# Attention's first head: the last projection of the first stage in the other pair of PSUM banks, and the head's finishing work in another order

## The chip, the cores and the metric

The kernel runs on one core of a Trainium2 chip. The core has five engines that work from their own queues, each in order: TensorE (PE, matrix products), VectorE (DVE), ScalarE (ACT), GpSimd (POOL) and SyncE (SP); the last two here mostly issue transfers (DMAs). Matrix products are accumulated in PSUM, which has eight banks of 512 float32 columns on 128 partitions. What is measured is the time of one execution in microseconds; lower is better.

## The reference

The program is one layer of a decoder for 512 tokens of width 2048: an RMS norm, attention with 16 heads of 128 in four groups, a residual add, a second norm, a SwiGLU feed-forward, and a last norm. The attention has three branches, compressed, selected and windowed, which are merged with gates:

```python
proj = h @ w_in
q, kc, vc, ks, vs, kw, vw, gl = jnp.split(proj, bounds, axis=-1)
...
s_c = jnp.einsum('btghd,bcgd->bghtc', q, kcc) + bias_c
p_c = masked_softmax(s_c, mask_c)
...
o = gates[0] * o_c + gates[1] * o_s + gates[2] * o_w
return o.reshape(Bsz, S, N_HEADS * DH) @ w_out
```

With 512 tokens the eight selection blocks are all chosen and the window spans the sequence, so that the selected and the windowed branch are two causal attentions over all tokens, each with its own keys and values, and the compressed branch has 31 keys.

## The kernel before

Every product is made of three (`three`): both factors are split in a high and a low part, ACT making the high part by a copy and DVE the low part by a subtraction. A weight granule, 512 KB, is loaded, split (`Weights.split`: ACT writes `whi`, DVE then `wlo`) and taken (`Weights.take`). A take keeps the splits three granules ahead and the loads three more; so each take issues one split and then one load, at that place of the program.

The first stage (pool `ps1`, with `psx` beside it that lives on) makes the compressed keys and values, the keys and values of group 0 and the queries of heads 0 and 1. Its projections take two PSUM tiles at a time, `proj_tiles`, from `psx` and `ps1` in turn. The last of them is that of the first queries: `q_out` scales each half on DVE (`yt`, L319), has ACT write the high part (`qh`, L292) and DVE the low part (`ql`, L293). After it `ps1` is closed, and `ps2` opens over the same banks with the score tile `s` (three banks), two tiles for projections and one for the output `o`.

The second stage (`st2`) goes head by head. For each head h there are four token tiles t, longest first:

- `scores(h, t)`: PE multiplies queries and keys into `s` (L267 to L269). DVE adds the bias and takes the maxima (L800, `mx`), ACT makes the exponentials (L802).
- `finish(h, t)`: DVE scales by the sums and gates (L807 to L814) and transposes in 32 x 32 blocks (L815); SP writes the tile to DRAM in four transfers (`d_p`).
- `fetch(t)`: reads it back into `ptr`, turned. For head 0 this is issued from POOL, from head 1 on from SP.
- `turn(h, b, kt)`: ACT (L838, `pth`) and DVE (L842, `ptl`) split one key tile of one branch.
- `values(h, b, kt)`: PE multiplies it with the values into `o`.

Beside this runs a stream of independent projections, `dense()`: the next queries, keys and values, in steps of three 512-column products, each counted as 650 ns. `pump(h, step)` issues steps until their sum reaches a goal that grows by 20800 ns a head, 12 pump steps to a head, with a lead of four of these. Eight steps use up one granule of the queries in each fourth: steps 1, 9, 17 and 25 take one, and step 28 and step 32 end the two halves of a pair of queries (`q_out`). The first pair of the stream lies in `psx`. Its weights are loaded from POOL's queue, that of the fetches of head 0.

Ahead of the loop over heads, head 0 is started by hand: four passes, each of a `scores`, a `fetch`, a `finish` and a `pump`. In the loop, steps 0 to 8 each `turn` one tile, steps 2 to 11 multiply what was turned two steps before, and `scores` and `finish` of the next head stand at every third step. The program's order is the order in each engine's queue.

Of the kernel before, what the change touches and what calls it, by code (L numbers as in the profile page):

```python
# [10 lines left out]
F32 = mybir.dt.float32  # L11
# [162 lines left out]
def nsa_block(ctx: ExitStack, tc: tile.TileContext, x, rel_bias, mix_g, ffn_g, fin_g, w_in, w_out,  # L174
              pos_k, w1k, w2k, pos_v, w1v, w2v, f_in, f_out, onehot, out):
    nc = tc.nc
    mm, act, dve, pool = nc.tensor.matmul, nc.scalar.activation, nc.vector, nc.gpsimd
# [9 lines left out]
    psx = early.enter_context(tc.tile_pool(name="psx", bufs=2, space=PSUM))  # L187
# [17 lines left out]
    def tok(t):  # L205
        return slice(128 * t, 128 * (t + 1))
# [59 lines left out]
    def three(o, ah, al, bh, bl, start, stop):  # L266
        mm(o, ah, bh, start=start, stop=False, skip_group_check=True)  # L267
        mm(o, ah, bl, start=False, stop=False, skip_group_check=True)  # L268
        mm(o, al, bh, start=False, stop=stop, skip_group_check=True)  # L269
# [80 lines left out]
    with ExitStack() as st1:  # L350
        ps1 = st1.enter_context(tc.tile_pool(name="ps1", bufs=2, space=PSUM))

        turns = iter(range(1000))

        def proj_tiles(n=2):
            return [(ps1 if next(turns) % 4 > 1 else psx).tile([128, 512], F32, name="proj") for _ in range(n)]

        c0p = st1.enter_context(tc.tile_pool(name="c0p", bufs=1))
        posT = c0p.tile([128, 2, 32], F32, name="posT")
# [2 lines left out]
        with ExitStack() as st0:  # L362
# [90 lines left out]
            for k in range(4):  # L453
                scaled_in(k, ps[k])
            ps = proj_tiles()
            for q in range(4):
                it = ws(ps, q, W.take(0))
# [92 lines left out]
        for u in range(2):  # L550
            kv_out(ps_kc0, 0)(u)
        ps = proj_tiles()
        for i in range(4):
            run(ws(ps, i, W.take(), end=kv_out(ps, 2)))
            next(spread)
        ps = proj_tiles()
        for i in range(4):
            run(ws(ps, i, W.take()))
# [71 lines left out]
    with ExitStack() as st2:  # L630
# [112 lines left out]
        STEPS = 12  # L743

        def pump(h, step):
            at = h + (step + 4) / STEPS
            goal = 20800 * min(at, 13) + 22500 * max(at - 13, 0)
            while done["ns"] < goal:
                c = next(stream, "end")
                if c == "end":  # L750
                    return
                done["ns"] += c or 0
# [15 lines left out]
        def load_bias(h):  # L768
            if h < H:
                TB[h] = ap_.tile([128, S], F32, name="tb")  # L770
                (nc.sync if h else pool).dma_start(TB[h], bass.AP(tensor=d_u.tensor, offset=d_u.offset + h * UL + 127,
                                                 ap=[[H * UL - 1, 128], [1, S]]))

        def branch(t, b):

            return P[t][:, :, 32 * (t + 1) * b:32 * (t + 1) * (b + 1)]

        def scores(h, t):
            g, n = h // HPG, 128 * (t + 1)
            (qh, ql), (kh, kl) = Q[h], KK[g % 2]  # L780
            if t == NT - 1:
                HS[h] = dict(
                    mx=ap_.tile([128, NT, 3], F32, name="mx"), sm=ap_.tile([128, NT, 3], F32, name="sm"))
            s = HS[h]
            at = 224 + (512 if t == 1 else 0)
            cuts = [0, 288] + [c for c in (800, 1056) if c <= 32 + 2 * n]
            if cuts[-1] < 32 + 2 * n:
                cuts.append(32 + 2 * n)
            for c0, c1 in zip(cuts, cuts[1:]):
                three(sc[:, at + c0:at + c1], qh[:, tok(t)], ql[:, tok(t)], kh[:, c0:c1], kl[:, c0:c1], True, True)  # L790
            c = CX[t][:, :NCMP]
            regions = [(c, c, c, sc[:, at:at + NCMP], biasc[:, h, 24 - 8 * t:24 - 8 * t + NCMP])]
            bt = TB[h][:, S - n:].rearrange("p (n s) -> p n s", s=128)
            sw = sc[:, at + 32:at + 32 + 2 * n].rearrange("p (n b s) -> p b n s", b=2, s=128)
            for b in range(2):
                u = ap_.tile([128, S], F32, name="u")[:, :n]
                regions.append((u.rearrange("p (n s) -> p n s", s=128), u.rearrange("p (n j s) -> p j n s", j=4, s=32),
                                branch(t, b).rearrange("p j (n s) -> p j n s", s=32), sw[:, b], bt))
            for i, (u, v, p, ps, bias) in enumerate(regions):
                dve.tensor_tensor_reduce(out=u, in0=ps, in1=bias, op0=OP.add, op1=OP.min, scale=-1.0,  # L800
                                         scalar=1e38, accum_out=s["mx"][:, t, i:i + 1])
                act(p, v, AF.Exp, bias=s["mx"][:, t, i:i + 1], scale=-1.0, accum_out=s["sm"][:, t, i:i + 1])  # L802
            s[t] = [c] + [branch(t, b) for b in range(2)]

        def finish(h, t):
            r = HS[h]["sm"][:, t]
            dve.reciprocal(r, r)  # L807
            dve.tensor_mul(r, r, gates[:, t, h])
            for i, p in enumerate(HS[h].pop(t)):
                o = p  # L810
                if not i:
                    o = P[t][:, :3, runs[t] - 32:]
                    p = CX[t].unsqueeze(1).to_broadcast([128, 3, 32])
                dve.tensor_scalar(o, p, r[:, i:i + 1], None, op0=OP.mult)  # L814
            dve.transpose(P[t], P[t])  # L815
            for i in range(4):
                nc.sync.dma_start(d_p[t][:, :, i].rearrange("j a r -> a j r"), P[t][32 * i:32 * (i + 1)])

        def fetch(t, queue=nc.sync):

            queue.dma_start(PT[:, :, PT_STEP * t:PT_STEP * t + runs[t]], d_p[t].rearrange("j a i r -> (j a) i r"))
# [46 lines left out]
        W.queue = pool  # L868
        load_bias(0)
        load_bias(1)  # L870
        for i in range(4):
            scores(0, 3 - i)
            if i > 1:
                fetch(5 - i, pool)
            if i:
                finish(0, 4 - i)
            pump(-1, min(9 + i, 11.7))
        for h in range(H):
            seq = [(b, kt) for kt in (3, 2, 1, 0) for b in (0, 1)] + [(-1, 0)]
            for i in range(STEPS):  # L880
                if i == 4:
                    load_bias(h + 2)
                if i == 2:
                    fetch(0, nc.sync if h else pool)
                if i < 9:
                    turn(h, *seq[i])
                if i == 8 and h + 1 < H:
                    fetch(3)
                    fetch(2)
                if i == 11 and h + 1 < H:  # L890
                    fetch(1)
                if i == 0:
                    if not h:
                        fetch(1, pool)
                    finish(h, 0)
                if h + 1 < H:
                    if i == 2:
                        drain_to(needed(h + 1))
                    if i % 3 == 2:
                        scores(h + 1, 3 - i // 3)  # L900
                    elif i % 3 == 0 and i:
                        finish(h + 1, 4 - i // 3)
                if 2 <= i < 10 or i == 11:
                    if i == 2 and h % HPG == 0:
                        drain_to(h)
                    values(h, *seq[min(i - 2, 8)])
                    if i == 11:
                        head_out(h)
                pump(h, i)
# [510 lines left out]
    n, na, pending = 0, 1, None  # L1420
# [88 lines left out]
```

## Time and profile before

| | |
|---|---|
| median of 3 runs | 2129.46 us (2128.89 to 2129.64) |
| profiled execution | 2127.83 us, span 2126.1 us |
| PE busy | 2099.3 us (99%) |
| DVE busy | 1634.5 us (77%) |
| ACT busy | 932.5 us (44%) |
| granted TensorE clock, mean | 0.997 |

Times are microseconds from the start of the span. A row of a timeline has the start, the duration, the engine, the line, the operation with its output and inputs, and in brackets the idle time of that engine just before it with what ended it. A row of a waits view names the engine and what it was about to write, the operation that released it, the total, the number of waits and the longest. `proj`, `s` and `o` are the PSUM tiles of projections, scores and outputs.

### The profile page before, as it was taken

Reading aid. Unit: us, or ns where it says so; the run is one execution under the profiler, and the core shown is the slowest. Engines: PE = TensorE matmul, PEld = TensorE weight load, DVE = VectorE, ACT = ScalarE, POOL = GpSimd, SP = SyncE. Lnnn points to the kernel's source line nnn. Section 1 sums busy time; section 2 is a strip of 40 time slices with the busy share of each in tenths; the row PEclk is TensorE's granted clock in tenths of the full one; section 3 lists DMA queues with packets and bytes.
Section 4 is the critical chain, followed back from the end, with each engine's and each line's share of the span. In section 5 each row is a group of like instructions: output and inputs, shape, how many; then the busy total and the mean of one; then the engine's idle time right before and its main releaser. Section 6 shows DMA issues by size and latency. Waiting matters only on the chain.

```text
span 2126.1 us, 37171 instructions
## 1 busy us (share of the span) xinstructions
PE 2099.3 (99%) x14697; PEld 1947.6 (92%) x14697; DVE 1634.5 (77%) x2670; ACT 932.5 (44%) x1447; POOL 125.8 (6%) x206
## 2 busy tenths in 40 slices
PE   9999999999999999999999999999999999999998
PEld 7898788898989889899999999999999888999996
DVE  5565777877786466898888888888888777877785
ACT  5344455555554334434334343443434444444344
POOL 1000111111111000000000000000000000001000
PEclk9999999999999999999999999999999999999999
DMA  7555667666676633444344343443333776878894
GB/s 228 180 151 151 192 193 201 184 200 188 199 233 203 240 140 109 128 131 129 120 129 129 120 126 123 129 127 122 123 124 122 273 274 213 302 271 309 307 335 143
DMA packets 272635, 388.08 MB, mean 183 GB/s; under 512 B 34155, under 2 KB 204715, under 8 KB 271820
## 3 DMA queue, kind: packets, MB, share of 16 engines
q1 hardware_dynamic: 247660, 279.19, 41.7%
q0 software_dynamic: 22896, 102.31, 13.9%
q10 hardware_dynamic: 1904, 4.20, 0.5%
q8 instruction: 115, 1.88, 0.4%
q14 instruction: 60, 0.49, 0.1%
HBM read 320.52 MB, written 70.36 MB: 184 GB/s over the span
## 4 chain that ended last, share of the span: by engine, by line
PE 68%; DVE 1%; DMA 1%; ACT 1%; issue 0%; ACTq 0%; DVEq 0%
PE f L268 19%; PE f L269 19%; PE f L267 19%; PE proj L267 2%; PE proj L269 2%; PE proj L268 2%; PE pp L267 1%; PE pp L269 1%; PE pp L268 1%; PE po L267 1%; PE po L268 1%; PE po L269 1%; DMA tt<-d_a 1%; PE pp L245 0%; DVE tlo L1008 0%
## 5 line engine op out<-in xcount | busy, mean ns | idle before, releaser
L98 DVE TENSOR_TENSOR wlo<-raw,whi 128x1024 fp32r<-128x1024 f32 (+1 forms) x226 | 270.8, 1200 | 114.5 <-ACT whi L97 114.3
L97 ACT ACTIVATE whi<-raw 128x1024 fp32r<-128x1024 f32 (+1 forms) x226 | 234.4, 1040 | 222.6 <-DVE raw L1008 123.7
L1008 DVE TENSOR_TENSOR tlo<-tt,thi 128x1536 fp32r<-128x1536 f32 (+2 forms) x135 | 197.2, 1460 | 109.2 <-ACT thi L1110 87.2
L267 PE MATMUL f<-hn_h,whi 128*128 128x256 f32 x984 | 272.0, 276 | 0.8 <-ACT E L1068 0.8
L268 PE MATMUL f<-hn_l,whi 128*128 128x256 f32 x984 | 271.9, 276 | 0.0
L269 PE MATMUL f<-hn_h,wlo 128*128 128x256 f32 x984 | 271.9, 276 | 0.0
L1105 ACT ACTIVATE whi<-raw 128x1024 fp32r<-128x1024 f32 x123 | 126.0, 1057 | 293.7 <-DVE raw L1008 283.5
L267 PE MATMUL proj<-hn_h,whi 128*128 128x512 f32 x512 | 204.3, 399 | 0.5 <-ACT hn_h L402 0.5
L268 PE MATMUL proj<-hn_l,whi 128*128 128x512 f32 x512 | 200.9, 392 | 0.3 <-DVE hn_l L403 0.3
L269 PE MATMUL proj<-hn_h,wlo 128*128 128x512 f32 x512 | 200.7, 392 | 0.0
L267 PEld LDWEIGHTS f<-hn_h,whi 128*128 128x128 f32 x984 | 184.8, 188 | 1.2 <-ACT E L1068 1.2
L269 PEld LDWEIGHTS f<-hn_h,wlo 128*128 128x128 f32 x984 | 184.7, 188 | 0.0
L268 PEld LDWEIGHTS f<-hn_l,whi 128*128 128x128 f32 x984 | 184.7, 188 | 0.0
L1110 ACT ACTIVATE thi<-tt 128x1536 fp32r<-128x1536 f32 x82 | 121.9, 1486 | 82.7 <-PE f L268 71.1
L269 PE MATMUL proj<-whi,hn_l 128*128 128x256 f32 (+2 forms) x496 | 146.3, 295 | 2.9 <-DVE hn_l L703 2.9
L1008 DVE TENSOR_TENSOR wlo<-raw,whi 128x1024 fp32r<-128x1024 f32 x123 | 147.1, 1223 | 1.1 <-ACT whi L1105 1.1
L267 PE MATMUL proj<-whi,hn_h 128*128 128x256 f32 (+2 forms) x496 | 146.6, 296 | 0.8 <-ACT hn_h L702 0.8
L268 PE MATMUL proj<-wlo,hn_h 128*128 128x256 f32 (+2 forms) x496 | 145.7, 294 | 0.0
L269 PE MATMUL f<-whi,tlo 128*128 128x512 f32 x320 | 125.0, 391 | 0.6 <-DVE tlo L1008 0.6
L268 PE MATMUL f<-wlo,thi 128*128 128x512 f32 x320 | 125.1, 391 | 0.3 <-DVE wlo L98 0.3
L267 PE MATMUL f<-whi,thi 128*128 128x512 f32 x320 | 124.8, 390 | 0.0
L269 PEld LDWEIGHTS proj<-hn_h,wlo 128*128 128x128 f32 x512 | 96.5, 189 | 21.5 <-DVE wlo L98 0.2
(327 smaller groups left out, 6104.7 us busy)
## 6 DMA issues: line engine op xcount, KB each, us to landing
raw<-in_ffn_w_in SPq DMA_DIRECT2D x135, 512.0 KB, 3.6
raw<-in_ffn_w_out SPq DMA_DIRECT2D x88, 512.0 KB, 6.0
rawx<-in_ffn_w_in SPq DMA_DIRECT2D x41, 512.0 KB, 4.9
rawx<-d_a SPq DMA_DIRECT2D x31, 512.0 KB, 4.9
ah<-d_s POOLq DMA_DIRECT2D x16, 896.0 KB, 7.2
al<-d_s POOLq DMA_DIRECT2D x16, 896.0 KB, 9.5
raw<-in_nsa_w_in SPq DMA_DIRECT2D x24, 512.0 KB, 4.6
raw<-in_nsa_w_in POOLq DMA_DIRECT2D x24, 512.0 KB, 4.8
```

The costliest lines, as they stand in the source:

```text
L97: self.nc.scalar.activation(hi[:, :n], src, AF.Copy)
L98: self.nc.vector.tensor_tensor(lo[:, :n], src, hi[:, :n].bitcast(F32), op=OP.subtract)
L267: mm(o, ah, bh, start=start, stop=False, skip_group_check=True)
L268: mm(o, ah, bl, start=False, stop=False, skip_group_check=True)
L269: mm(o, al, bh, start=False, stop=stop, skip_group_check=True)
L1008: dve.tensor_tensor(o, a, b, op=OP.subtract)
L1105: act(h, r, AF.Copy)
L1110: act(h, ttf, AF.Copy)
```

## The change

The projection tiles' turn is mirrored: where a pair came from `psx`, it now comes from `ps1`, and the other way round. The first queries' projection, the last, so comes to lie in `psx`, and the stream's first pair, also in `psx`, follows it there.

`pump` has a lead of five steps up to the start of head 0, and this falls evenly to four at the start of head 1.

Head 0's start is written out. `finish(0, 3)` stands ahead of `scores(0, 2)`; `finish(0, 2)` and `finish(0, 1)` stand, as before, behind the scores of the next tile, but now ahead of the fetch in the same pass. The pumps between them ask for 2, 10, 12 and 14 steps in all; before it was 3, 6, 8 and 10.

```diff
         def proj_tiles(n=2):
-            return [(ps1 if next(turns) % 4 > 1 else psx).tile([128, 512], F32, name="proj") for _ in range(n)]
+            return [(psx if next(turns) % 4 > 1 else ps1).tile([128, 512], F32, name="proj") for _ in range(n)]
...
         def pump(h, step):
-            at = h + (step + 4) / STEPS
+            at = h + step / STEPS
+            at += (4 + min(max(1 - at, 0), 1)) / STEPS
             goal = 20800 * min(at, 13) + 22500 * max(at - 13, 0)
...
         load_bias(1)
-        for i in range(4):
-            scores(0, 3 - i)
-            if i > 1:
-                fetch(5 - i, pool)
-            if i:
-                finish(0, 4 - i)
-            pump(-1, min(9 + i, 11.7))
+        scores(0, 3)
+        pump(-1, 7.5)
+        finish(0, 3)
+        scores(0, 2)
+        pump(-1, 10.5)
+        scores(0, 1)
+        finish(0, 2)
+        fetch(3, pool)
+        pump(-1, 11.2)
+        scores(0, 0)
+        finish(0, 1)
+        fetch(2, pool)
+        pump(-1, 11.9)
         for h in range(H):
```

## The prediction

> **What bounds the kernel now.** I read the totals first: TensorE (PE) is busy for all but some 27 us, so only its gaps can be won. Then its waits, from 180 to 300 us, where the change lies.
>
> ```profile
> PE 2099.3 (99%) x14697; PEld 1947.6 (92%) x14697; DVE 1634.5 (77%) x2670; ACT 932.5 (44%) x1447; POOL 125.8 (6%) x206
> ...
> PE o L267 <- issue: 3.0, 1, 3.0
> PE s L267 <- DVE yt L319: 1.7, 1, 1.7
> PE s L267 <- DVE mx L800: 0.8, 1, 0.8
> ```
>
> These are all of its gaps there, 5.5 us. The table by stretches, for this place and for one near 610 us, shows what a gap costs afterwards (columns: stretch, length, busy time of PE, PEld, DVE, ACT and POOL, granted clock, DMA).
>
> ```profile
> 200.00:204.00 4.00, 2.28 (x12) 1.68 (x11) 2.52 (x3) 2.11 (x3) 0.02 (x1) 1.00 0.69 203
> 220.00:224.00 4.00, 1.50 (x6) 1.26 (x7) 1.39 (x7) 0.51 (x2) 2.33 (x4) 0.93 0.96 299
> 224.00:228.00 4.00, 4.00 (x14) 3.27 (x14) 2.33 (x9) 2.31 (x8) 0.68 (x1) 0.64 0.75 225
> ...
> 608.00:612.00 4.00, 1.84 (x16) 1.64 (x14) 3.78 (x9) 1.98 (x3) 0.00 (x0) 1.00 1.03 346
> 612.00:616.00 4.00, 4.00 (x19) 3.77 (x20) 2.44 (x9) 2.80 (x9) 0.00 (x0) 0.57 0.93 282
> ```
>
> The gap of 1.7 us (200:204) left the clock at 1.00. The one of 3.0 was followed by a clock of 0.64 for 4 us, and 2.16 us of idleness (608:612) by 0.57. Such a dip costs 4 x 0.43 = 1.7 us at 612, and (1 - 0.64) x 4 + 0.07 x 4 = 1.7 here. So at most 5.5 + 1.7 = 7.2 us can be won, 0.34%.
>
> Next I followed VectorE (DVE) and ScalarE (ACT) through head 0. One piece of a `finish` or a `turn` waits for ACT, ACT for a maximum of DVE, and neither waits for PE: after 212 us this pair runs at its own pace, and PE follows with little to spare. The row that shows it is the last `turn` with three products, ready on DVE at 240.28 + 0.68 = 240.96; PE used it at 241.92.
>
> ```profile
> 240.28 0.68 DVE L842 TENSOR_TENSOR ptl<-ptr,pth 128x512 fp32r<-128x512 f32 x1
> ...
> 241.92 0.39 PE L268 MATMUL o<-ptl,v0h 128*128 128x512 f32 x1
> ```
>
> That leaves 0.9 us. Whatever delays the DVE/ACT pair in head 0 by more than this delays PE. That is my measure for the change.
>
> **Part 1, the bank pair.** The turn in `proj_tiles` is mirrored. In the first stage every pair of tiles meets the same predecessors as before, mirrored, so I cost that at nothing. Only the last pair differs: it no longer lies in the pool that the score tile replaces. The readers of what lies there now stand in DVE's queue ahead of the queries' own, so `scores(0, 3)` goes at 201.76 (203.48 less its gap of 1.72). The filler's first steps write the queries' banks instead: the first bank's reader ends at 199.17 + 0.69, and the second bank is needed only by step 5, after the next wait.
>
> ```profile
> 203.48 0.37 PE L267 MATMUL s<-k0h,qh 128*128 128x288 f32 x1 [1.72 <-DVE yt L319]
> 205.00 0.39 PE L267 MATMUL proj<-hn_h,whi 128*128 128x512 f32 x1
> 207.07 0.29 PE L267 MATMUL s<-k0h,qh 128*128 128x288 f32 x1
> ...
> 199.17 0.69 DVE L319 SCALAR_TENSOR_TENSOR yt<-proj,ybc 128x512 f32<-128x512 f32 x1
> 204.03 0.69 DVE L293 TENSOR_TENSOR ql<-yt,qh 128x512 fp32r<-128x512 f32 x1 [0.70 <-ACT qh L292]
> 205.31 0.19 DVE L800 CUSTOM_DVE_ANT_0 cx<-s,biasc 128x31 f32<-128x31 f32 x1 [0.58 <-PE s L269]
> 206.67 0.08 DVE L800 DVE_READ_ACCUMULATOR2_ANT mx<- 128x1 f32 x1
> ```
>
> But DVE reduces the scores only after `ql`, at 204.7 (205.31 less the idle 0.58) instead of 205.31: 0.6 us earlier. PE has 1.5 us of scores and two filler steps (three took 2.07, so 0.69 each) and reaches `scores(0, 2)` at 204.7. Scores wait for the maxima of the tile before (the 0.8 us row above), and the last maximum of tile 3 is out at 206.75 - 0.6 = 206.15. So the 1.7 us come back as 1.4. What is late next is DVE.
>
> **Part 2, the finishes forward.** These rows hold DVE's pieces; the start of the next piece ends one.
>
> ```profile
> 208.45 0.19 DVE L800 CUSTOM_DVE_ANT_0 cx<-s,biasc 128x31 f32<-128x31 f32 x1 [1.70 <-PE s L269]
> 209.53 0.17 DVE L807 RECIPROCAL sm<-sm 128x3 f32<-128x3 f32 x1
> 212.34 0.15 DVE L800 CUSTOM_DVE_ANT_0 cx<-s,biasc 128x31 f32<-128x31 f32 x1
> 213.12 0.17 DVE L807 RECIPROCAL sm<-sm 128x3 f32<-128x3 f32 x1
> 215.53 0.15 DVE L800 CUSTOM_DVE_ANT_0 cx<-s,biasc 128x31 f32<-128x31 f32 x1
> 218.04 1.18 DVE L98 TENSOR_TENSOR wlo<-raw,whi 128x1024 fp32r<-128x1024 f32 x1
> ...
> 207.57 0.19 ACT L802 ACTIVATION_READ_ACCUMULATOR p<-u,mx 128x1 f32 x1
> 210.35 0.19 ACT L802 ACTIVATION_READ_ACCUMULATOR p<-u,mx 128x1 f32 x1
> 216.82 1.04 ACT L97 ACTIVATE whi<-raw 128x1024 fp32r<-128x1024 f32 x1
> ...
> 217.09 0.77 POOL L821 DMA_DIRECT2D ptr<-d_p  x1 [17.07 <-DMA d_p<-p]
> 220.09 0.76 POOL L821 DMA_DIRECT2D ptr<-d_p  x1 [2.23 <-DMA d_p<-p]
> 220.83 1.52 POOL L81 DMA_DIRECT2D raw<-in_nsa_w_in  x2
> ...
> 222.10 0.51 ACT L838 ACTIVATE pth<-ptr 128x128 fp32r<-128x128 f32 x2 [4.23 <-DMA ptr<-d_p]
> 224.84 0.42 ACT L838 ACTIVATE pth<-ptr 128x256 fp32r<-128x256 f32 x1 [2.23 <-DMA ptr<-d_p]
> ```
>
> The maxima of tile 2 take 209.53 - 208.45 = 1.08, finish of tile 3 takes 2.81, maxima of tile 1 0.78, finish of tile 2 2.41. New order: finish of tile 3 starts when its exponentials are out, 207.76 - 0.6 = 207.15, and ends at 209.95, 2.4 us earlier than before. Maxima of tile 2 end at 211.0. Then comes what the new lead moved: `pump(-1, 10.5)` asks for 6067 ns, ten steps of 650, and the ninth takes the next weight granule and so splits one and loads one. Before, the ninth stood in the last pump, behind everything (the split at 218.04, the load at 220.83). Now the split stands ahead of the maxima of tile 1. Its ACT half waits for the exponentials of tile 2, out 2.09 after those maxima began (210.54 against 208.45), at 212.05; 1.05 of ACT and 1.2 of DVE give 214.3. DVE sits idle for 2.0 of that. Maxima of tile 1 end at 215.1, finish of tile 2 at 217.5: 1.95 us later than the 215.53 of before.
>
> The moved load also stands ahead of `fetch(3)` on POOL: it must wait for the split (214.3, and some 0.4 to issue) and takes 1.5, so `fetch(3)` goes at 216.1, not when its data are ready (217.09 - 2.4 = 214.7). It was used 5.0 us after its issue; that gives 221.1, one us earlier than 222.10. `fetch(2)` was used 224.84 - 215.53 = 9.3 us after finish of tile 2; that gives 226.8. No row shows it without the 512 KB load that stood beside it (220.83) and now does not; I put its gain at 0 to 1 us and take 0.5. So the second tile's `turn` comes at 226.3, 1.5 later than before, and all that is behind it in DVE and ACT with it, the maxima of head 1 first.
>
> **Part 3, five steps of lead.** It gives PE filler in head 0 sooner (16 steps instead of 14 ahead of the first product with values), but every step brings its weight split along, now ahead of `turn` and `finish` in the two queues.
>
> ```profile
> 225.63 0.18 DVE L800 CUSTOM_DVE_ANT_0 cx<-s,biasc 128x31 f32<-128x31 f32 x1
> 231.54 1.18 DVE L98 TENSOR_TENSOR wlo<-raw,whi 128x1024 fp32r<-128x1024 f32 x1
> 232.65 1.01 DVE L842 TENSOR_TENSOR ptl<-ptr,pth 128x384 fp32r<-128x384 f32 x2
> 233.58 0.18 DVE L800 CUSTOM_DVE_ANT_0 cx<-s,biasc 128x31 f32<-128x31 f32 x1
> 240.88 0.69 DVE L319 SCALAR_TENSOR_TENSOR yt<-proj,ybc 128x512 f32<-128x512 f32 x1
> 242.27 0.69 DVE L293 TENSOR_TENSOR ql<-yt,qh 128x512 fp32r<-128x512 f32 x1 [0.70 <-ACT qh L292]
> ...
> 227.95 0.40 ACT L838 ACTIVATE pth<-ptr 128x256 fp32r<-128x256 f32 x1
> 235.50 0.62 ACT L838 ACTIVATE pth<-ptr 128x512 fp32r<-128x512 f32 x1
> ```
>
> Let X be the start of the maxima of head 1's tile 3 (225.63 before). Step 17, with a split, moves from behind `finish(1, 3)` to ahead of it and of a `turn`. ACT is free at X + 2.32 (227.95), its half ends at X + 3.37, DVE's at X + 4.53; then a turn of some 0.34 (256 columns, between the 0.3 of 128 and the 0.6 of 512), finish 2.81, two turns 0.93 (232.65 to 233.58): maxima of tile 2 at X + 8.62, where they stood at X + 7.95. That is 0.67 later. From there (Y, 233.58 before), the last turn came at 240.28, Y + 6.70. Now a split goes first (ACT free at Y + 1.92, from 235.50; its half out at 2.97, DVE's at 4.13), then a turn 0.6 (240.28 to 240.88), finish 2.41, and the queries of step 28, which moved ahead of the last turn as well (240.88 to 242.27 and 0.6 more: 2.0): Y + 9.16. That is 2.46 later. PE had 0.9 to spare there and has done one step more (33, not 32), 0.69.
>
> Sum for PE: 1.5 + 0.67 + 2.46 - 0.9 - 0.69 = 3.0 us later. The gaps of before and their dip are inside this, since it compares clock times at equal work. Head 1 on has the same order, lead and spare (one split, at step 41, moves ahead of a turn that could wait), so the 3.0 neither grow nor shrink.
>
> **The dip.** The turn two before comes out at X + 8.2. After it PE has seven steps (4.8) and 5088 columns of other products (2.3 at 0.69 for 1536) up to the last turn's product, so it is there at X + 15.3. That turn starts on DVE at 0.67 + 7.95 + 9.16, X + 17.8, its ACT half just before, and is out 0.7 later: PE idles some 2.4 and 0.6 us with one product between, more than the 2.16 that was followed by a dip at 612. Bounds: 0 (the 1.7 us gap had none) and 1.7; I take 1.7, as the longer rows are nearer. A dip after the earlier, shorter gaps would be eaten by the next wait. Sum: 3.0 + 1.7 = 4.7 us.
>
> [...]
>
> **Against the runs.** The profiled execution took 2127.83 us (span 2126.1); the median of the runs is 2129.46, 1.63 above. 2127.83 + 4.7 = 2132.5, and beside the median 2134.2, or +0.22%. A measurement of this kernel tells about 0.2%, 4.3 us, from no change.
>
> **The rivals.** *No dip.* All as above, but the clock holds: 2129.46 + 3.0 = 2132.5. For it speaks the 1.7 us gap that had none, against it the other two rows.
> *The lead covers it (faster).* PE, not the DVE/ACT pair, sets the pace, and what counts is `fetch(3)`. Its product comes 1.0 earlier with two more steps done (1.4), and without the dip of before (1.7): 4.1 us. Should the moved load not hold POOL, `fetch(3)` is 1.4 earlier still, 5.5. Middle 4.8, so 2124.7. It decides if X comes before 225.63 - (3.0 - 1.5) = 224.1, where the loss is zero; that needs `fetch(2)` used 5.8 us after finish of tile 2, not 9.3. I see no row for that.
> *The waits only move.* `fetch(2)`, free of the load, lands a us or more sooner than taken, and PE's loss falls to 1 or less, with no dip: 2130.5.
>
> **How the numbers follow.** Forecast 0.52, no dip 0.22, waits only move 0.12, faster 0.10, and 0.04 for two dips (2136 and more). Of the forecast's 0.52 about three quarters lie beyond +4.3 us, since the 0 to 1 us of `fetch(2)` puts it between 4.2 and 5.2. Slower by over 0.2%: 0.39 + 0.02 + 0.04, with some for errors of DVE durations, 0.47. Within: 0.43. Faster: 0.10. The range goes from 2129.0, the waits that move with some to spare, to 2136.5, the dip with `fetch(2)` late by one us more and some drift; the forecast's own is 2133 to 2135.5.
>
> **What would show it.** Right: the wait of `s` on `yt` gone and one of some 1.4 on `mx` in its place; the finish of tile 3 ending near 210 and that of tile 2 near 217.5; a split on DVE between them; `fetch(3)` behind a weight load on POOL; several waits of `o` on `ptl` or `pth` between 220 and 246, the longest at the last 512-column turn, and a clock below 1 behind it. Wrong: if no `o` waits after 228, or DVE's turns of head 0 come no later than before.

## The result, and the profile after

The changed kernel takes 2134.22 us (median of 16 runs, 2131.06 to 2136.87). The kernel before, run on the same chip between them, takes 2129.54 (16 runs, 2127.60 to 2132.42). The ratio is 1.0020, with a 95% interval of 1.0014 to 1.0027: 4.7 us slower. The profiled execution took 2132.14 us (span 2130.4), 4.3 more than that of before.

The first view is the page of the changed kernel with its totals, then its waits of TensorE from 180 to 300 us.

```profile
PE 2102.4 (99%) x14697; PEld 1947.8 (91%) x14697; DVE 1635.3 (77%) x2670; ACT 933.2 (44%) x1447; POOL 126.2 (6%) x206
...
PE o L268 <- DVE ptl L843: 2.9, 3, 1.6
PE o L267 <- issue: 2.1, 1, 2.1
PE o L267 <- ACT pth L839: 2.0, 1, 2.0
PE s L267 <- DVE mx L801: 1.6, 1, 1.6
```

The wait of `s` on `yt` is gone, one on `mx` stands in its place, and 4.9 us of waits of `o` on `ptl` and `pth` are new. In all there are 8.6 us of gaps, where there were 5.5. The next fence is the timeline of the same kernel: DVE's pieces, then POOL's transfers, ACT's first halves of the turns, and PE's first products behind a wait. (Lines below the change stand one further down than before: `turn`'s low part is L843, the transposition L816.)

```profile
210.01 0.15 DVE L801 CUSTOM_DVE_ANT_0 cx<-s,biasc 128x31 f32<-128x31 f32 x1
213.04 1.23 DVE L98 TENSOR_TENSOR wlo<-raw,whi 128x1024 fp32r<-128x1024 f32 x1 [1.91 <-ACT whi L97]
216.63 1.11 DVE L816 STREAM_TRANSPOSE p<-p 128x896 f32<-128x896 f32 x1
217.67 0.15 DVE L801 CUSTOM_DVE_ANT_0 cx<-s,biasc 128x31 f32<-128x31 f32 x1
228.60 0.18 DVE L801 CUSTOM_DVE_ANT_0 cx<-s,biasc 128x31 f32<-128x31 f32 x1
237.66 0.18 DVE L801 CUSTOM_DVE_ANT_0 cx<-s,biasc 128x31 f32<-128x31 f32 x1
246.77 0.68 DVE L843 TENSOR_TENSOR ptl<-ptr,pth 128x512 fp32r<-128x512 f32 x1
...
214.56 1.55 POOL L81 DMA_DIRECT2D raw<-in_nsa_w_in  x2 [14.52 <-DVE mx L801]
216.11 0.79 POOL L822 DMA_DIRECT2D ptr<-d_p  x1
223.59 0.75 POOL L822 DMA_DIRECT2D ptr<-d_p  x1 [6.69 <-DMA d_p<-p]
...
221.71 0.51 ACT L839 ACTIVATE pth<-ptr 128x128 fp32r<-128x128 f32 x2 [2.66 <-DMA ptr<-d_p]
227.81 0.42 ACT L839 ACTIVATE pth<-ptr 128x256 fp32r<-128x256 f32 x1 [5.59 <-DMA ptr<-d_p]
...
206.13 0.40 PE L267 MATMUL s<-k0h,qh 128*128 128x288 f32 x1 [1.55 <-DVE mx L801]
246.70 0.50 PE L267 MATMUL o<-pth,v0h 128*128 128x512 f32 x1 [1.96 <-ACT pth L839]
251.91 0.40 PE L854 MATMUL o<-pth,vcc 96*128 96x512 f32 x1
```

Two points of this timeline serve as measures from here on. The **mark** is the last row: the first head's product with the compressed values (`vcc`). When PE reaches it, 38 filler steps have been issued in every kernel of this study, so it compares times at equal work. **X** is what the prediction calls so, the start of the maxima of head 1's tile 3, at 228.60. In the kernel before, X was 225.63, and its mark and the transposition of tile 2, from the timeline of that kernel, were these:

```profile
214.50 1.11 DVE L815 STREAM_TRANSPOSE p<-p 128x896 f32<-128x896 f32 x1
...
246.88 0.40 PE L853 MATMUL o<-pth,vcc 96*128 96x512 f32 x1
```

So X came 3.0 us later and the mark 5.0 us later. Behind the mark the difference drifts by about one microsecond each way: it is 5.9 us at the first product of the feed-forward (880.31 and 886.17), and 4.3 at the end.

One more place in the kernel before matters below: PE's scores just ahead of the mark (second row), and the maxima on DVE that must be out before them (first row).

```profile
245.18 0.19 DVE L800 CUSTOM_DVE_ANT_0 cx<-s,biasc 128x31 f32<-128x31 f32 x1
...
246.50 0.29 PE L267 MATMUL s<-k0h,qh 128*128 128x288 f32 x1
```

The table by stretches of the changed kernel, with the columns as in the prediction, shows one dip of the clock, behind the first gap, and none behind the last turn at 246.70:

```profile
220.00:224.00 4.00, 1.90 (x7) 1.59 (x7) 2.03 (x9) 0.51 (x2) 0.41 (x1) 0.81 0.68 199
224.00:228.00 4.00, 4.00 (x17) 3.14 (x15) 0.19 (x2) 0.19 (x1) 1.09 (x2) 0.77 0.75 218
...
244.00:248.00 4.00, 1.73 (x7) 0.89 (x6) 3.13 (x5) 2.50 (x4) 0.00 (x0) 1.00 0.82 232
248.00:252.00 4.00, 4.00 (x21) 3.33 (x20) 3.20 (x10) 2.08 (x8) 0.76 (x1) 1.00 0.32 60
```

### The profile page after: what moved, and what is told of

Its sections match the earlier page's. It is cut to its first block, busy times and chain, and to the rows that moved or that the text cites. A ratio compares the mean times of both kernels' runs of the same rounds, so it can differ in the third digit from the quotient of the medians.

```text
span 2130.4 us, 37177 instructions
## 1 busy us (share of the span) xinstructions
PE 2102.4 (99%) x14697; PEld 1947.8 (91%) x14697; DVE 1635.3 (77%) x2670; ACT 933.2 (44%) x1447; POOL 126.2 (6%) x206
## 4 chain that ended last, share of the span: by engine, by line
PE 68%; DVE 1%; ACT 1%; DMA 0%; issue 0%; ACTq 0%; DVEq 0%
PE f L268 19%; PE f L269 19%; PE f L267 19%; PE proj L267 2%; PE proj L269 2%; PE proj L268 2%; PE pp L267 1%; PE pp L268 1%; PE pp L269 1%; PE po L267 1%; PE po L269 1%; PE po L268 1%; DMA tt<-d_a 0%; PE pp L245 0%; DVE tlo L1015 0%
```

## The experiments

The theory: three things delay the pair of DVE and ACT in head 0, each on its own, and PE behind it. These are the split and load of the ninth step, ahead of the maxima of tile 1 and of `fetch(3)`; the trip of tile 2 to DRAM and back; and, inside the loop over heads, the splits and query pieces that the lead brings ahead of the turns. The rivals: the start alone does it (then a start as before with the new lead costs nothing), the bank pair does it, or the wait that moves explains all.

The table gathers what was measured. "Mark" and "X" are shifts against the kernel before, less the shift of the last `yt` of the first queries on DVE (it starts at 202.65 before and differs by up to 0.3 us, in e7 by 1.8; e9 moves it and isn't corrected). "Trip" is the time from the end of tile 2's transposition to the issue of `fetch(2)`, that is, its write to DRAM; "gap" is the time from the issue of `fetch(3)` to the end of that transposition (negative: `fetch(3)` goes later). The ratios are those on record, estimated from all runs, and need not equal the quotient of the two medians. Mark, X, gap and trip are from one execution each.

| kernel | median and ratio [95%] to before | mark | X | gap | trip |
|---|---|---|---|---|---|
| before | | 0 | 0 | -1.5 | 4.5 |
| changed | 2134.22, 1.0020 [1.0014, 1.0027] | +5.0 | +2.9 | +1.6 | 5.9 |
| e11, changed again | 2134.27, one execution | +6.9 | +3.6 | +1.7 | 6.8 |
| e1, banks alone | 2128.05, 0.9997 [0.9987, 1.0007] | +0.5 | -0.4 | -1.5 | 4.4 |
| e2, lead of four | 2130.87, 1.0012 [1.0003, 1.0021] | +2.4 | +2.6 | +1.6 | 5.5 |
| e10, lead of four, split late | 2127.30, one execution | +1.1 | +1.4 | +1.1 | 6.1 |
| e3, split late | 2132.80, 1.0020 [1.0010, 1.0029] | +5.0 | +1.7 | +1.1 | 6.3 |
| e4, load late | 2132.54, 1.0019 [1.0009, 1.0028] | +5.0 | +1.4 | +2.7 | 4.4 |
| e5, order alone | 2129.62, 1.0009 [1.0000, 1.0018] | +1.9 | +2.2 | +0.9 | 6.5 |
| e6, lead alone | 2134.30, 1.0036 [1.0024, 1.0047] | +8.2 | +4.5 | -0.2 | 6.5 |
| e7, lead with splits in place | 2129.34, 1.0009 [1.0000, 1.0019] | +1.1 | +1.3 | +1.1 | 6.1 |
| e8, finishes in a pair | 2125.78, 0.9996 [0.9987, 1.0005] | -2.1 | -1.9 | -2.3 | 4.4 |
| e9, as e8, first split later | 2127.01, 0.9997 [0.9988, 1.0006] | -1.5 | -1.2 | -2.1 | 4.4 |
| e12, e8 again | 2125.92, 0.9991 [0.9982, 1.0000] | -1.4 | -1.2 | -2.3 | 4.3 |

The kernel before took 2128.64 beside e1 to e4, 2127.41 beside e5 to e8 and 2128.13 beside e9 to e12.

**e1: the bank pair alone.** Of the change only this line is made, against the kernel before:

```diff
-            return [(ps1 if next(turns) % 4 > 1 else psx).tile([128, 512], F32, name="proj") for _ in range(n)]
+            return [(psx if next(turns) % 4 > 1 else ps1).tile([128, 512], F32, name="proj") for _ in range(n)]
```

> The kernel before with the mirrored banks alone. The mark in all runs is the start of head 0's compressed product (o<-pth,vcc), where 38 filler steps are done: 246.9 us before, 251.9 after the change. Theory (in head 0 the queue of VectorE and ScalarE sets TensorE's time): the scores of tile 3 are reduced 0.6 earlier and those of tile 2 at 207.5 instead of 208.45, so all that VectorE does up to the last finish, and both fetches, come 0.9 earlier and the mark at about 246.0. Rival (the waits only move): the wait on yt becomes one on mx of about 0.9, later ones grow by as much, and the mark stays at 246.9.

The time doesn't change. The timeline and the stretches of e1:

```profile
222.08 0.44 PE L267 MATMUL o<-pth,v0h 128*128 128x128 f32 x1 [3.37 <-issue]
...
247.44 0.40 PE L853 MATMUL o<-pth,vcc 96*128 96x512 f32 x1
...
220.00:224.00 4.00, 1.92 (x6) 1.73 (x7) 1.81 (x8) 0.51 (x2) 2.03 (x4) 0.64 0.98 320
224.00:228.00 4.00, 4.00 (x13) 3.23 (x12) 1.91 (x8) 2.62 (x9) 0.27 (x1) 0.51 0.63 169
```

The wait on `yt` is gone, and DVE's chain is 0.4 us earlier. But PE, now ahead of it, waits longer for the first product with values (3.4 us for 3.0), and the clock dips to 0.64 and 0.51. What the bank pair wins at 204 is lost at 222, and the mark, 247.4, is nearer the rival's 246.9 than the theory's 246.0; the bank pair isn't the cause of the loss either.

**e2: the changed start with the old lead.** `pump` is as before, and the goals of the start are shifted so that it issues the same steps at the same places as the changed kernel. Against the changed kernel:

```diff
-            at = h + step / STEPS
-            at += (4 + min(max(1 - at, 0), 1)) / STEPS
+            at = h + (step + 4) / STEPS
...
-        pump(-1, 7.5)
+        pump(-1, 8.5)
```

(and so on, 11.5, 12.2 and 12.9 for the others)

> The changed kernel, its start with the same 2, 10, 12 and 14 steps, but a lead of four steps within the loop over heads. Theory: from head 1's tile 3 on, the splits stand behind finish and turn again, as before; those maxima start at 228.6 as in the changed kernel, the last 512-column turn starts on VectorE some 14.7 later instead of 18.2, and the mark comes 2.5 to 3 earlier than in the changed kernel, at 249.0 to 249.5. Rival (TensorE lacks filler at the first fetch, and what costs is that gap and the clock dip behind it): with 14 instead of 16 steps of cover the gap at the first product is 1.4 longer, and the mark is at 252 or later.

The mark, from e2's timeline, is at 249.53; above it are the scores just ahead of it and the maxima that they wait for:

```profile
248.08 0.19 DVE L800 CUSTOM_DVE_ANT_0 cx<-s,biasc 128x31 f32<-128x31 f32 x1
...
249.03 0.40 PE L267 MATMUL s<-k0h,qh 128*128 128x288 f32 x1
249.53 0.40 PE L853 MATMUL o<-pth,vcc 96*128 96x512 f32 x1
```

X is nearly where the changed kernel has it, but the mark is 2.6 us earlier. So the start costs 2.4 us and the lead inside the loop 2.6 more, as the theory has it. No wait is left here at the last turn; what holds PE just ahead of the mark are the maxima of head 1's tile 1. The mark comes 1.45 us after these start (248.08 to 249.53), where it came 1.70 after them before (245.18 to 246.88).

**e10: as e2, with the ninth step in the last pump.** The start's goals end at 2, 8, 8 and 14 steps, so that the split and the load stand behind everything, as before. Against e2:

```diff
         scores(0, 2)
-        pump(-1, 11.5)
+        pump(-1, 10.9)
...
-        pump(-1, 12.2)
+        pump(-1, 10.9)
```

> The changed kernel with 2, 8, 8 and 14 steps in its start (the split of step 9 behind the last finish) and a lead of four in the loop. Theory A: what is left of the change is its order and its banks; fetch(2) is used at 226.6 as in the run with the late split, the maxima of head 1's tile 3 start at 227.4, no piece of the loop is moved, and the mark is 0.2 us less late than these, 1.5 us later than before the change, at 248.3 to 248.6. Rival (the lead in the loop costs nothing by itself, the late split did not help because of dips): mark at 250 or later.

Its timeline, with the transposition of tile 2, the two fetches and the mark:

```profile
214.81 1.11 DVE L815 STREAM_TRANSPOSE p<-p 128x896 f32<-128x896 f32 x1
...
214.85 0.77 POOL L821 DMA_DIRECT2D ptr<-d_p  x1 [14.70 <-DMA d_p<-p]
222.01 0.76 POOL L821 DMA_DIRECT2D ptr<-d_p  x1 [6.39 <-DMA d_p<-p]
...
248.15 0.40 PE L853 MATMUL o<-pth,vcc 96*128 96x512 f32 x1
```

The mark comes 1.3 us ahead of e2's: that is what the early split costs. `fetch(3)` goes 2.2 us earlier than before (214.85 for 217.09) and the finish of tile 2 ends 0.3 later. Still `fetch(2)` goes 1.9 us later (222.01 for 220.09), because the write of tile 2 took 6.1 us (214.81 + 1.11 = 215.92 to 222.01) where it took 4.5 (215.61 to 220.09). These 1.6 us account for what is left of the start's loss.

**e3: the changed kernel with the ninth step late.** The same start as e10, but with the lead of five inside the loop. Against the changed kernel:

```diff
-        pump(-1, 10.5)
+        pump(-1, 9.9)
...
-        pump(-1, 11.2)
+        pump(-1, 9.9)
```

> The changed kernel with 2, 8, 8 and 14 steps in its start instead of 2, 10, 12 and 14, so that step 9 with its split and its load stands behind the last finish of the start, as before the change. Theory: finish of tile 2 ends at 215.6 instead of 217.7, fetch(3) goes at 214.7 and is used at 219.7 to 220.2, fetch(2) is used at 224.8 to 226.0 instead of 227.8; the reordering in the loop still costs its 3.1; the mark comes 2 to 3 earlier, at 249 to 250. Rival (only the gap at the first fetch and its dip count): fetch(3) is covered, the dip is gone, and the mark is below 247.

X is 1.2 us earlier than in the changed kernel, but the mark isn't, and the time neither: a miss. Part of it is `fetch(2)`, used at 226.59 instead of 224.8 to 226.0, since the write of tile 2 took 6.3 us. The stretches of e3 around the last turn show where the rest of the gain went.

```profile
244.00:248.00 4.00, 2.40 (x5) 1.62 (x6) 3.10 (x5) 2.62 (x4) 0.00 (x0) 0.70 0.57 157
248.00:252.00 4.00, 4.00 (x18) 3.27 (x18) 3.15 (x13) 1.96 (x7) 0.76 (x1) 0.87 0.60 158
```

Here the clock dips behind the gap of the last turn, which the profiled execution of the changed kernel had without a dip. It costs (1 - 0.70) x 4 + (1 - 0.87) x 4 = 1.7 us. Against e10, which has the same start, the lead costs 3.9 at the mark: 2.6 as between e2 and the changed kernel, and 1.3 for the dip. Against e11 (below), the changed kernel in an execution with this dip, the mark of e3 is 1.9 us earlier, as its X is.

**e4: the changed kernel with the load alone held back.** The split stays where it is; the loads wait until after the last `fetch` of the start. Against the changed kernel:

```diff
+        W.hold = True
         pump(-1, 10.5)
...
         fetch(2, pool)
+        W.hold = False
+        W.ahead(0)
```

(`Weights.ahead` and `take` load nothing while `hold` stands)

> The changed kernel with the split of step 9 where it is, but the load that goes with it issued from POOL only behind fetch(2). Theory (the split on VectorE delays fetch(2); the load adds to it): fetch(3) is issued at 214.7 and used at 219.8; if the load is what made the write of tile 2 take 5.9 us to its fetch instead of 4.5, fetch(2) is issued at 222.2 and used at 226.5 to 227.0, and the mark is at 250.6 to 251.1. Rival (the load is the whole delay of fetch(2)): used at 225.0 and the mark at 249. If the load has no part in it: fetch(2) used at 227.8, mark 251.9.

The two fetches in e4's timeline:

```profile
214.88 0.77 POOL L823 DMA_DIRECT2D ptr<-d_p  x1 [14.70 <-DMA d_p<-p]
222.00 0.76 POOL L823 DMA_DIRECT2D ptr<-d_p  x1 [6.35 <-DMA d_p<-p]
```

Without the load ahead, `fetch(3)` goes 1.2 us earlier. It is far ahead of the write of tile 2, which can begin at 217.62, when its transposition ends; the data of `fetch(3)` are used 1.7 us after that (219.34), and the write takes 4.4 us again. X gains 1.5 us on the changed kernel, as expected. The mark missed its expectation, again by a dip behind the last turn (0.75 and 0.83 in the stretches from 244 to 252).

**e5: the order of the finishes alone.** Banks and lead as before; the goals of the start are those of before (3, 6, 8 and 10 steps).

```diff
-        for i in range(4):
...
+        scores(0, 3)
+        pump(-1, 9)
+        finish(0, 3)
+        scores(0, 2)
+        pump(-1, 10)
...
```

> The kernel before (old banks, lead of four, the same 3, 6, 8 and 10 steps in its start) with the finishes of head 0 in the order of the change. Mark as before: start of head 0's compressed product, 246.9 us before and 251.9 after the change. Theory A (the transfer of tile 2 sets the queue of VectorE and ScalarE, and its write to DRAM takes some 4.4 us up to the issue of its fetch when it is issued clear of fetch(3), 5.5 to 6.3 when it follows fetch(3) by 1 to 2 us, as the runs with the changed order showed): fetch(3) is issued at 215.3, the write of tile 2 follows 0.9 later, fetch(2) is issued at 221.5 to 222.2 and used at 226 to 226.7 instead of 224.8, and the mark is at 247.5 to 248.0, with or without a gap more. Rival (the earlier first fetch helps): used 1.8 earlier than before at 220.3, the gap there shrinks and the mark is at 246 or below.

The mark is 1.9 us late and the time 2.2 us, at the edge of its interval. The trip of tile 2 accounts for 2.0 us of it, at 6.5 us with no load near it: the ninth step isn't needed for the slow write. The expected mark, 247.5 to 248.0, was about 1 us too early (249.02), since the trip was put at 5.5 to 6.3.

**e6: the lead alone.** Only `pump` is changed; the loop of the start and the banks are as before.

```diff
-            at = h + (step + 4) / STEPS
+            at = h + step / STEPS
+            at += (4 + min(max(1 - at, 0), 1)) / STEPS
```

> The kernel before with the changed lead alone (6, 8, 11 and 13 steps in its start). Theory A: fetch(3) is used at about 222.1 and fetch(2) at 225 to 226; two more steps cover the first fetch, so the gap there is 1.7 instead of 3.0, but splits and the queries' last pieces stand ahead of the turns, the last 512-column turn starts on VectorE 17 to 18.2 behind the maxima of head 1's tile 3 instead of 14.7, and the mark is at 248.4 to 249.5. Rival (steps of lead are cover): the mark is 1.4 to 3 earlier than before, at 244 to 245.5.

It is the slowest of all, +6.9 us, and far from its expectation: the mark is at 255.18. One step more than meant fell into the second pump (the goal was just above eight steps), so that the ninth step's load stands ahead of both fetches, as e6's timeline shows:

```profile
215.98 1.54 POOL L81 DMA_DIRECT2D raw<-in_nsa_w_in  x2 [15.85 <-DVE mx L801]
219.35 0.75 POOL L822 DMA_DIRECT2D ptr<-d_p  x1 [1.82 <-DMA d_p<-p]
```

X is 4.5 us late and the loop adds 3.7, with a clock of 0.79 behind the last turn. So the old order of the start with the new lead is worse than both together, and the order isn't needed for the loop's loss. But with the ninth step moved this start isn't that of before, so that e6 is no clean test of the rival that the start alone does it; that rests on e2 and e7. How the 4.5 divide between split, load and write wasn't separated.

**e7: the lead kept, the splits left where they were.** The start of e3 and the lead of five, but the filler's takes no longer split ahead; the splits and loads are issued by hand at the places where the kernel before has them, and the step that ends a query half stays behind the last turn.

```diff
-                last = ws(ps, i, W.take(), end=end)
+                last = ws(ps, i, W.take(0 if h0 == 2 else 2), end=end)
...
+                if not h and i in (3, 6):
+                    W.upto(base + 5 + i // 6)
-                pump(h, i)
+                pump(h, 5.5 if not h and i == 6 else i)
```

(`W.upto(k)` splits up to granule k and loads three more; it also stands once behind the last `fetch` of the start)

> The changed kernel with 2, 8, 8 and 14 steps in its start, the lead of five, but the three splits of head 0 (with their loads) and the end of the first half of its queries at the places of the program where the kernel before has them. Theory A: the last 512-column turn starts some 14.7 behind the maxima of head 1's tile 3, which start at 227.4 as in the run with the late split (fetch(2) used at 226.6); the turn starts at 242.1, the mark is at 247.0, 4.9 earlier than in the changed kernel and where it was before the change. Rival (the lead itself, by the products' place among the filler, delays): the mark stays above 249.5.

The whole stage starts 1.8 us later in this execution (the last `yt` of the first queries at 204.48 for 202.65). As it stands the mark, 249.79, is past the rival's 249.5. With the late start taken off, the mark is at +1.1 where e3, with the same start and the same filler for PE, has +5.0. So the lead itself is free; the work that it brings along in DVE's and ACT's queues costs the 2.6 us (and the dip). It missed its expectation by 1 us; X is late by 1.3, and the trip of tile 2 (6.1 us) accounts for it.

A comparison over all kernels says the same without a correction. From X to the mark it takes 20.97 to 21.02 us in each of the seven kernels that have the old lead in the loop or the splits in place, and a changed start (e2, e5, e7, e8, e9, e10 and e12), though e5, e7 and e10 have a dip of the clock in that stretch and the others none. In the kernel before it takes 21.25, in e1, with a dip twice as long, 22.1; in the changed kernel 23.3 without a dip at the last turn, and 24.5 to 24.9 with one (e11, e3, e4 and e6). So behind X it is the queue of DVE and ACT that sets PE's time, and the lead's extra work costs 2.3 us of it, or 3.5 to 3.9 with the dip that its wait brings.

**e8 and e12: both finishes behind the scores of tile 2.** From these readings: the finishes of tiles 3 and 2 follow each other, ahead of the maxima of tile 1, `fetch(3)` stands behind these, the splits stay in place as in e7, and the lead is written as a list of steps.

```diff
+        scores(0, 3)
+        fill(3)
+        scores(0, 2)
+        finish(0, 3)
+        finish(0, 2)
+        fill(11)
+        scores(0, 1)
+        fetch(3, pool)
+        fill(14)
+        scores(0, 0)
+        finish(0, 1)
+        fetch(2, pool)
+        W.upto(base + 4)
+        fill(16)
```

(in head 0's loop `fill` goes to 17, 21, 22, 24, 25, 27, 27, 31, 33, 36, 38 and 40 steps; from head 1 on `pump` is as before)

> The mirrored banks, with another start: scores of tiles 3 and 2, then both their finishes, then scores and finish of the others; the splits where the kernel before has them; and the filler counted out by hand (3, 11, 14 and 16 steps in the start, 21 ahead of the first product with values, 33 ahead of the last turn's). Theory A: finish of tile 3 ends at 211.5 and of tile 2 at 213.9, fetch(3) is issued at 216.1 and used at 221.1, fetch(2) at 218.3 and used at 223.1, the maxima of head 1's tile 3 start at 223.9, 1.7 earlier than before, and the mark is at 244.8 to 245.3, 1.6 to 2.1 earlier than before. Rival (TensorE's gaps, which move elsewhere, decide): the mark is at 246.5 or later.

> The version with the finishes of tiles 3 and 2 as a pair once more, with more rounds, since its 2125.78 against 2127.41 us left open whether it is faster than the kernel before. Theory A: the mark at 244.9 and the time 1.5 to 2.5 us below the kernel before, 0.07 to 0.12%.

The timeline and stretches of e8:

```profile
231.53 0.44 PE L274 MATMUL o<-ptl,v0h 128*128 128x384 f32 x1 [2.22 <-DVE ptl L854]
...
244.90 0.40 PE L865 MATMUL o<-pth,vcc 96*128 96x512 f32 x1
...
228.00:232.00 4.00, 1.78 (x9) 1.23 (x9) 3.97 (x9) 0.94 (x2) 0.54 (x1) 1.00 0.47 111
232.00:236.00 4.00, 4.00 (x23) 3.52 (x23) 2.50 (x12) 3.71 (x9) 0.95 (x2) 1.00 0.96 280
```

The write of tile 2 is ahead of `fetch(3)` again and takes 4.4 us, X is 1.9 us earlier than before, no wait for the first product with values is left, and the mark is 2.1 us earlier than that of before (1.4 in e12). The time is 1.6 and 2.2 us under that of before; the intervals reach to 1.0005 and to 1.0000, so it is at best a gain at the edge of what can be measured.

**e9: as e8, with one split of the first stage later.** The split that stands between the halves of the first queries' projection moves behind both.

```diff
-            if end and gi == 3 and u:
+            if end and gi == 3 and u and h0:
                 W.ahead(3)
```

(`h0` is 0 for the first queries alone)

> The version with the finishes of tiles 3 and 2 as a pair, and in it the last weight split of the first stage (1.1 us of VectorE between the two halves of the first queries, with its load) moved behind the start of head 0. Theory A (the queue of VectorE and ScalarE sets the time): the maxima of tile 3 start at about 203.9 instead of 204.8 and everything up to the mark follows, the maxima of head 1's tile 3 at 223.0 and the mark at 244.0 to 244.3, 2.6 to 2.9 earlier than the 246.9 of the kernel before. Rival (that version is bound by something else, TensorE or the transfers): mark unchanged at 244.9.

DVE begins the first maxima 1.0 us earlier than in e12 (203.77 for 204.77), but the filler now waits for its weights, as e9's timeline shows:

```profile
217.77 0.50 PE L273 MATMUL proj<-hn_h,whi 128*128 128x512 f32 x1 [1.17 <-ACT whi L97]
219.15 0.50 PE L275 MATMUL proj<-hn_h,wlo 128*128 128x512 f32 x1 [0.64 <-DVE wlo L98]
```

The mark (245.39 for an expected 244.0 to 244.3) lies between those of e8 and e12: the 1 us is given back.

**e11: the changed kernel once more.** No edit.

> The changed kernel as it is, for a second profile. The first one has no dip of the clock behind the wait at the last 512-column turn (2.0 and 0.3 us), while two runs with like waits there had one. If a dip there is a matter of the moment, this profile may show one, with the mark 1.2 to 1.6 later than in the first, 253.1 to 253.5; without one it is at 251.9 again.

This execution took 2134.27 us, by chance that of the median. Its timeline (transposition of tile 2, `fetch(2)`, X, last turn, mark) and its stretches:

```profile
216.55 1.12 DVE L816 STREAM_TRANSPOSE p<-p 128x896 f32<-128x896 f32 x1
...
224.46 0.75 POOL L822 DMA_DIRECT2D ptr<-d_p  x1 [7.64 <-DMA d_p<-p]
...
229.17 0.18 DVE L801 CUSTOM_DVE_ANT_0 cx<-s,biasc 128x31 f32<-128x31 f32 x1
...
247.27 0.62 PE L267 MATMUL o<-pth,v0h 128*128 128x512 f32 x1 [2.01 <-ACT pth L839]
...
253.76 0.40 PE L854 MATMUL o<-pth,vcc 96*128 96x512 f32 x1
...
244.00:248.00 4.00, 1.89 (x7) 0.90 (x5) 3.27 (x5) 1.93 (x3) 0.00 (x0) 0.94 0.78 220
248.00:252.00 4.00, 3.92 (x11) 3.15 (x12) 3.42 (x10) 2.28 (x9) 0.76 (x1) 0.64 0.27 55
```

The same gap as at 246.70 in the first profile (2.0 us, here 247.27) is followed by a dip this time, 0.06 x 4 + 0.36 x 4 = 1.7 us of clock. The mark is 1.85 us later than in the first profile: 0.57 from X (the write of tile 2 took 6.8 us here) and 1.3 from the dip.

## Why the prediction was right, and where not

The forecast, 2134.2 with +4.7 us, is the measured one (2134.22, +4.7). Its steps are not all as good as its sum.

**Part 1** held. The wait on `yt` came back as 1.55 us on `mx` (1.4 forecast).

**Part 2** held up to `fetch(3)`: the finish of tile 3 ended at 210.01 (209.95), the split at 214.2 (214.3), the finish of tile 2 at 217.67 (217.5), the load went at 214.56, `fetch(3)` at 216.11 (216.1) and was used at 221.71 (221.1). Then one step failed: "`fetch(2)` was used 9.3 us after finish of tile 2; I put its gain at 0 to 1 us and take 0.5". It was used 10.1 us after it (217.67 to 227.81), and 10.8 in e11: a loss of 0.8 to 1.5, outside both bounds. I had looked at the 512 KB load that would no longer stand beside `fetch(2)`. I had not seen that the write of tile 2, which before ran ahead of `fetch(3)`, now comes 1.6 us behind it and takes 5.9 us instead of 4.5. So X was 228.60, not 227.1, and the term "1.5 later" measured 2.9.

**The measure**, 0.9 us of slack at the last turn, held where the last turn decides: in the changed kernel that turn started 6.49 us later (240.28 and 246.77), and less 0.9 and 0.69 this gives 4.9 for the 5.0 at the mark. But it wasn't the tightest row. The scores just ahead of the mark had only 0.25 us to spare behind the maxima of head 1's tile 1 (e2), so that the kernels with the old lead lose nearly all that X loses.

**Part 3** held in its durations. The maxima of tile 2 came at X + 9.06 (8.62), and the last turn 9.11 after them (9.16). Its size is confirmed by e2, which has the start without the lead: 2.6 us less at the mark (0.3 of it stands in X), where 0.67 + 2.46 - 0.69 = 2.4 was the sum before the slack. e7 shows that the cause is the one named, splits and query pieces ahead of the turns.

**The sum without the dip** was 3.0, and the mark shows 5.0. Of the 2.0 us missing, 1.5 stand in X (1.3 of them from the end of the finish of tile 2 to the use of `fetch(2)`) and 0.4 between X and the last turn.

**The dip** at the last turn was there in one of the two profiles, with the gap that was forecast (2.0 and 0.2 to 0.3 us; forecast 2.4 and 0.6). e3, e4 and e6, with the same lead, have it too. It cost 1.3 at the mark of e11, for 1.7. So the rival "no dip" can hold in an execution and not in the next. The prediction chose between them by the length of the gap, and that doesn't settle it (see the last section): its size for a dip, 1.7, was right, and its presence was a bet. Four of the five profiles with this lead at this place had it; the first profiled execution, 2.1 us under the median, is the one without.

With the write and with a dip the mark is late by 6.9, not 4.7. By medians the loss is 4.7. "The 3.0 neither grow nor shrink" from head 1 on is only right within 1 to 2 us: in the first profile 5.0 at the mark became 5.9 and then 4.3 at the end, in e11 6.9 became 6.6 and 6.4. And the profiled execution of before is itself 1.7 us under its median, so 4.3 and 6.4, from single executions, stand on a low base. That the forecast meets the median to 0.1 us is thus partly luck: two errors cancel, an X that was put 1.5 us too early and a drift that isn't explained.

**The rivals.** "The lead covers it" fell: X came at 228.60, and its condition was 224.1. "The waits only move" describes e1, the bank pair alone, but not the whole.

## What to carry to other kernels

A TensorE that is 99% busy can still be paced by another pair of engines in one stretch: find there the rows with the least slack (here the one found first had 0.9 us and a later one 0.25), and weigh each edit by what it puts ahead of the critical pieces in those queues. More lead for a filler isn't free if each of its steps brings preparing work along (here 2.3 us behind X): keep the preparation at its old place (e7) or cost it there. And where a transfer is moved, look not only at what no longer runs beside it but at what now runs ahead of it (here the same write took 4.5 us ahead of a read-back and 5.9 behind it).

## What the runs showed of the hardware

**The write of tile 2 took longer where the read-back was issued close to it.** The column "trip" of the table sorts by the column "gap". Where `fetch(3)` (576 KB) was issued 1.5 to 2.3 us after the write of tile 2 could begin, or 2.7 us ahead of it, the write took 4.3 to 4.5 us (before, e1, e8, e9, e12 and e4). Where it was issued between 0.2 us after and 1.7 us ahead, it took 5.5 to 6.8 us (changed, e2, e3, e5, e6, e7, e10, e11), with or without a weight load near it. The writes are issued from SP and the fetches from POOL, so neither stands behind the other in an engine's queue. In the changed kernel the DMA engines were 0.94 to 0.99 busy in each microsecond from 218 to 221, between the issue of `fetch(3)` at 216.11 and that of `fetch(2)` at 223.59. What makes the write slower was not shown, since no run moves the read-back alone by steps.

**The clock's dip doesn't go by the length of the gap alone.** The four gaps of 2.9 to 3.4 us all had a dip. But one of 1.8 us had a clock of 0.57 behind it (e5) and one of 1.5 us 0.76 and 0.82 (e7), while 2.2 us (e8) and 2.3 us (e4, e12) had 1.00, and the same gap of 2.0 had none in one execution and 0.64 in the other. The rows of e5:

```profile
227.71 0.39 PE L267 MATMUL o<-pth,v0h 128*128 128x256 f32 x1 [1.82 <-ACT pth L838]
...
228.00:232.00 4.00, 3.93 (x12) 3.10 (x12) 2.59 (x12) 3.49 (x9) 0.75 (x1) 0.57 0.57 167
```

The cost of a dip varies less. In stretches of 0.1 us the dip in the kernel before is a clock of 0.50 from 223.44 to 226.85, and the one in the changed kernel the same from 222.45 to 225.86: 3.4 us each, which costs 1.7 us. By stretches of 4 us the dips of e3, e4, e5, e7, e10 and e11 and the first of e6 cost 1.7 us each as well, and that of e1 3.4 (0.64 and 0.51 from 220 to 228).

Of the ten gaps of 1.9 to 2.1 us between 200 and 252 us in these profiles seven had a dip. What decides whether one follows was not shown.
